# Combining two expert outputs a token: weighted sums on TensorE through diagonal matrices instead of on VectorE

## Chip, core and metric

The kernel runs on one NeuronCore of a Trainium2 chip. The metric is the device time of one execution in microseconds (us). A tile is 128 tokens on the 128 partitions; there are eight tiles of 128 x 1024 fp32 values.

## The reference, cut to what matters

A decoder trunk of two layers works on 1024 tokens of width 1024. Each layer has a token mixer (a gated delta rule in layer 0, differential attention in layer 1) and then a mixture of experts, in which every token goes to two of 32 experts. Behind each comes a layer norm of the scaled residual stream:

```python
ALPHA = (2 * DEPTH) ** 0.25
def layer_norm(x, g, b):
    mu = jnp.mean(xf, axis=-1, keepdims=True)
    var = jnp.mean(jnp.square(xf - mu), axis=-1, keepdims=True)
    return ((xf - mu) * lax.rsqrt(var + LN_EPS) * g + b).astype(x.dtype)
...
    y = jax.ops.segment_sum(y_rows * row_gate[:, None], row_tok, num_segments=n)
...
    ffn = hierarchical_moe(h, moe_w_group[layer], moe_w_expert[layer], moe_w13[layer], moe_w2[layer])
    h = layer_norm(ALPHA * h + ffn, ln_ffn_g[layer], ln_ffn_b[layer])
```

For a token with the expert rows y0 and y1 and the gates g0 and g1 the part around the change computes layer_norm(ALPHA * h + g0 * y0 + g1 * y1).

## The kernel before

The program runs layer 0's mixer and experts, then `combine` (L1796) for layer 0, then the projections and the attention of layer 1, its output projection and experts, and at the very end `combine` for layer 1, whose output is the kernel's. The experts write their rows to a buffer `y` in HBM (two rows a token) by indirect DMA; an overflow loop behind them (L1769), whose number of trips is read at run time, ends every engine's work of the stage. `combine` starts behind it.

For each tile `combine` loads `yin`, the two expert rows of its tokens (1 MB, on SyncE's queue, three tiles ahead in layer 0, all eight in layer 1: `YB`), and for the later tiles the residual `h`. `first` has ScalarE multiply y0 by its gate (L1823); VectorE adds ALPHA * h (L1826) and then g1 * y1 (L1827), all in SBUF. `normalize` takes the statistics on VectorE (two `bn_stats` L245, `bn_aggr` L247), the reciprocal standard deviation on ScalarE with six activations of one column (`rstd`, L232 to L237: a logarithm and an exponential among them), and two passes: way 0 has both on VectorE (L258, L263); way 1 has the first on VectorE (L258), the scaling on ScalarE (L260) and the addition on GpSimd (L261); way 2 has one pass on ScalarE (L254) and two on GpSimd (L255, L256). `WAYS` gives the way of each tile: in layer 0 six tiles of way 1 and two of way 0; in layer 1 ways 1 and 2 in turn, then two of way 0.

ScalarE evaluates functions from a table, which an ACT_TABLE_LOAD brings in. `preload_act_table_set` (L1825) loads the set that holds both logarithm and exponential. Where an activation's set isn't known to be there, the compiler puts a load of its own ahead of it, on the activation's line.

In layer 0 each finished tile is stored to HBM (L1833) and also transposed: TensorE transposes it in eight pieces into PSUM (`ctr`, L1839), ScalarE copies them to `hT` (L1842), rounded, and VectorE writes the remainder (L1843). From tile 2 on `c.bp.start` begins projection units of layer 1 (`pj`, three matmuls in a row, L223 to L225, from `hT` and the split weights `wh` and `wl`), whose matmuls stand between the transposes on TensorE. The third unit is the first that needs all eight tiles of `hT`. A scheduler writes each engine's order at build time; each engine works its row in order.

Of the kernel before, what the change touches and what calls it, by code (L numbers as in the profile page):

```python
# [9 lines left out]
F32 = mybir.dt.float32  # L10
# [4 lines left out]
AF = mybir.ActivationFunctionType  # L15
OP = mybir.AluOpType
AX = mybir.AxisListType
PSUM = bass.MemoryType.PSUM

P = 128  # L20
D = 1024
T = 1024
KT = 8
NT = 8
# [3 lines left out]
ALPHA = 4.0 ** 0.25  # L28
# [23 lines left out]
CAH = 1  # L52

HA = ((2, 5), (2, 5))
YB = (3, 8)
LGT = 1
WAYS = ((1,) * 6 + (0,) * 2, (1,) * 6 + (0,) * 2, (1,) * 6 + (0,) * 2, (1, 2, 1, 2, 1, 2, 0, 0))
WB = 2
CAPS = (
    (96, 96, 80, 128, 128, 112, 112, 104, 96, 96, 88, 88, 80, 80, 80, 80) + (64,) * 8 + (56,) * 3 + (48,) * 5,  # L60
# [70 lines left out]
def instruction(i):  # L131
    return getattr(i, "ins", i)


def row_bc(ap, n):
    return bass.AP(tensor=ap.tensor, offset=ap.offset, ap=[[0, P], [1, n]])
# [91 lines left out]
def rstd(c, sd, mv):  # L228

    act = c.nc.scalar.activation  # L230
    r, v, w = (sd[:, i:i + 1] for i in range(3))
    act(w, mv[:, 1:2], AF.Ln, bias=c.ln_eps, scale=1.0)  # L232
    act(v, mv[:, 1:2], AF.Identity, bias=c.half_eps, scale=-0.5)
    act(r, w, AF.Exp, scale=-0.5)
    act(w, r, AF.Square)
    act(w, w, AF.Identity, bias=c.three_half, scale=v)  # L236
    act(r, r, AF.Copy, scale=w)  # L237


def normalize(c, lp, a, lg, lb, way):  # L240

    nc = c.nc
    st = lp.tile([P, 2, 6], F32, name="ln_st")
    for k in range(2):
        nc.vector.bn_stats(st[:, k, :], a[:, k * 512:(k + 1) * 512])  # L245
    mv = lp.tile([P, 2], F32, name="ln_mv")
    nc.vector.bn_aggr(mv, st)  # L247
    sd = lp.tile([P, 4], F32, name="ln_sd")
    rstd(c, sd, mv)
    r, m = sd[:, 0:1], sd[:, 3:4]  # L250
    if way == 2:
        nc.scalar.activation(m, mv[:, 0:1], AF.Copy, scale=-1.0)
        nc.scalar.activation(m, m, AF.Copy, scale=r)
        nc.scalar.activation(a, a, AF.Identity, scale=r, bias=m)  # L254
        nc.gpsimd.tensor_tensor(a, a, lg, OP.mult)  # L255
        nc.gpsimd.tensor_tensor(a, a, lb, OP.add)  # L256
        return
    nc.vector.scalar_tensor_tensor(a, a, mv[:, 0:1], lg, op0=OP.subtract, op1=OP.mult)  # L258
    if way == 1:
        nc.scalar.activation(a, a, AF.Copy, scale=r)  # L260
        nc.gpsimd.tensor_tensor(a, a, lb, OP.add)  # L261
    else:
        nc.vector.scalar_tensor_tensor(a, a, r, lb, op0=OP.mult, op1=OP.add)  # L263
# [573 lines left out]
def out_proj(c, res, part, layer, h_dram):  # L837
# [4 lines left out]
    with ExitStack() as es:  # L842
# [41 lines left out]
        def norm(n, t, a):  # L884
            normalize(c, lp, a, lg, lb, WAYS[layer][n])
            nc.sync.dma_start(h_dram[t * P:(t + 1) * P], a)
# [909 lines left out]
def combine(c, layer, h_dram, y_dram, dst, hT=None):  # L1796

    nc, tc, ins = c.nc, c.tc, c.ins
    with ExitStack() as es:
        yp = es.enter_context(tc.tile_pool(reuse_waits="tile", name="c_y", bufs=YB[layer]))  # L1800
        lp = es.enter_context(tc.tile_pool(reuse_waits="tile", name="c_l", bufs=3))
        ps = es.enter_context(tc.tile_pool(reuse_waits="tile", name="c_ps", bufs=2, space=PSUM))
        lg, lb = c.w.tile(), c.w.tile()
        c.h += [c.w.spare() for t in range(HA[layer][1], NT)]
        yv = y_dram.rearrange("(t p k) f -> t p k f", p=P, k=2)

        ys = []

        def load(t):

            ys.append(yp.tile([P, 2, D], F32, name="yin"))
            with tc.issue_after(c.load0) if t else ExitStack():
                c.load0 = instruction(nc.sync.dma_start(ys[t], yv[t]))
                if t == LGT:
                    nc.sync.dma_start(lg, row_bc(ins["ln_ffn_g"][layer], D))
                    nc.sync.dma_start(lb, row_bc(ins["ln_ffn_b"][layer], D))
                if t >= HA[layer][1]:
                    nc.sync.dma_start(c.h[t], h_dram[t * P:(t + 1) * P])

        def first(t):  # L1820
            n = TILES[layer].index(t)
            y, a = ys[t], c.h[t]
            nc.scalar.activation(y[:, 0], y[:, 0], AF.Copy, scale=c.gates[:, n, 0:1])  # L1823
            if t == 0:
                tc.keep_in_program_order(nc.scalar.preload_act_table_set("natural_log_exp_and_others"))  # L1825
            nc.vector.scalar_tensor_tensor(a, a, ALPHA, y[:, 0], op0=OP.mult, op1=OP.add)  # L1826
            nc.vector.scalar_tensor_tensor(a, y[:, 1], c.gates[:, n, 1:2], a, op0=OP.mult, op1=OP.add)  # L1827
            return t, a

        def second(t, a):  # L1830
            normalize(c, lp, a, lg, lb, WAYS[2 + layer][t])
            store = nc.gpsimd if layer == 0 and WAYS[2][t] else nc.sync
            store.dma_start(dst[t * P:(t + 1) * P], a)  # L1833
            if hT is not None:
                for gr in range(2):
                    pt = ps.tile([P, 4, P], F32, name="ctr")
                    for i in range(4):
                        k = gr * 4 + i
                        nc.tensor.transpose(pt[:, i], a[:, k * P:(k + 1) * P], c.ident)  # L1839
                    sl = slice(t * P, (t + 1) * P)  # L1840
                    kk = slice(gr * 4, gr * 4 + 4)
                    nc.scalar.copy(hT[0][:, kk, sl], pt)  # L1842
                    nc.vector.tensor_tensor(hT[1][:, kk, sl], pt, hT[0][:, kk, sl].bitcast(F32), OP.subtract)  # L1843


        for t in range(NT):
            while len(ys) < min(NT, t + YB[layer]):
                load(len(ys))
            second(*first(t))
            if layer == 0 and t >= WB:  # L1850
                c.bp.start(t - WB)
    c.raw2.close()
# [25 lines left out]
def build(c, out):  # L1878
    nc, tc = c.nc, c.tc
    with ExitStack() as es:  # L1880
# [11 lines left out]
        with ExitStack() as ws:  # L1892
            phase_a(c, ws, p1, h1)
            with ExitStack() as ms:
                experts_open(c, ms)
                routing(c, 0)
                c.first_b = [c.ins["w_kvq"][i] for i in (0, 16, 8)]
                experts(c, 0, h1, y1)
            bs = es.enter_context(ExitStack())
            hp = bs.enter_context(tc.tile_pool(reuse_waits="tile", name="hT", bufs=1))  # L1900
            hT = [hp.tile([P, KT, T], F32R, tag=f"hT{i}", name=f"hT{i}") for i in range(2)]
            ps = bs.enter_context(ExitStack())
            phase_b_open(c, ps)
            combine(c, 0, h1, y1, h2, hT)
        phase_b_attention(c, hT, hp, h2, p2)
        ps.close()
        with ExitStack() as ws:
            weights_open(c, 1, ws)
            out_proj(c, h2, p2, 1, h3)
            bs.close()  # L1910
            with ExitStack() as ms:
                experts_open(c, ms)
                routing(c, 1)
                experts(c, 1, h3, y2)
            combine(c, 1, h3, y2, out)
# [18 lines left out]
```

## Time and profile before

| | before |
|---|---|
| median of 3 runs | 2745.63 us (2743.77 to 2754.32) |
| profiled execution | 2752.11 us, of which span 2750.3 us |
| mean granted TensorE clock of it | 0.931 |
| TensorE busy | 2366.5 us, 86% of the span |
| VectorE busy | 1503.0 us, 55% |
| ScalarE busy | 1214.9 us, 44% |
| GpSimd busy | 545.2 us, 20% |
| stretch of `combine`, layer 0 | about 1364 to 1444 us |
| stretch of `combine`, layer 1 | about 2688 us to the end |

In the rows PE is TensorE, DVE is VectorE, ACT is ScalarE, POOL is GpSimd, SP is SyncE. A row of a timeline has the start, the duration (both in us, from the span's start), engine, line, operation and tiles written and read; xN joins N instructions. In brackets stands the idle time ahead of it and what ended that. The clock is a share of 2.4 GHz: 1.00 is 2.4 GHz and 0.50 is 1.2 GHz. An fp32 matmul leaves two records.

### The profile page before, as it was taken

The numbers are of one execution on the slowest core, as the hardware profiler recorded it, in microseconds if no ns is written. First come the engines' busy times: TensorE is split into PE (matmuls) and PEld (weight loads), VectorE is DVE, ScalarE is ACT, GpSimd is POOL, SyncE is SP. The second block draws the span as 40 slices with busy tenths as digits, with TensorE's granted clock in tenths as the row PEclk, the third lists the DMA queues.
The fourth block names the chain that finished last, engine by engine and source line by source line (L and its number), as shares of the span: only waits on it lengthen the run. The fifth ranks groups of instructions, "written<-read, shape, count | busy, mean of one in ns | idle before, by whom it ended". The sixth has DMA issues, their size and how long they took to land. (4 is left out here: it accounts for less than half of the span.)

```text
span 2750.3 us, 40132 instructions
## 1 busy us (share of the span) xinstructions
PE 2366.5 (86%) x14447; PEld 1645.2 (60%) x14447; DVE 1503.0 (55%) x2710; ACT 1214.9 (44%) x2187; POOL 545.2 (20%) x445
## 2 busy tenths in 40 slices
PE   8999999998979989898649999999886796779990
PEld 5777777776745544444238777777664373455560
DVE  4555555564556555455295667667535422334467
ACT  5355555543325444444255555556332322223454
POOL 3333333331212111010042111111012111111104
PEclk9999999999979999999859999999987898899995
DMA  4111111124678999999951110101445969799995
GB/s 145 51 59 51 55 59 47 58 75 123 242 274 302 394 388 381 383 380 384 351 210 35 39 33 31 39 26 61 155 170 210 393 250 363 288 381 362 362 366 230
DMA packets 195484, 564.09 MB, mean 205 GB/s; under 512 B 40400, under 2 KB 63184, under 8 KB 193232
## 3 DMA queue, kind: packets, MB, share of 16 engines
q1 hardware_dynamic: 178240, 515.07, 51.0%
q0 software_dynamic: 15168, 43.01, 4.5%
q10 hardware_dynamic: 1872, 3.40, 0.4%
q8 instruction: 115, 1.88, 0.3%
q14 instruction: 89, 0.73, 0.1%
HBM read 515.58 MB, written 52.89 MB: 207 GB/s over the span
## 5 line engine op out<-in xcount | busy, mean ns | idle before, releaser
L210 DVE TENSOR_TENSOR ml<-mraw,mh 128x1024 fp32r<-128x1024 f32 x300 | 357.0, 1222 | 289.4 <-ACT mh L210 270.5
L210 ACT CAST mh<-mraw 128x1024 fp32r<-128x1024 f32 x300 | 306.7, 1052 | 281.7 <-DMA mraw<-in_w 226.1
L210 PE MATMUL acc<-mh,xT 128*128 128x512 f32 (+5 forms) x976 | 331.8, 409 | 1.6 <-ACT mh L210 1.6
L210 PE MATMUL acc<-mraw,xTw 128*32 128x256 f32 (+1 forms) x1632 | 241.4, 500 | 18.7 <-DVE xTw L210 10.1
L185 POOL TENSOR_TENSOR wl<-raw,wh 128x512 fp32r<-128x512 f32 x106 | 155.0, 1482 | 485.1 <-ACT wh L184 420.9
L210 PEld LDWEIGHTS acc<-mh,xT 128*128 128x128 f32 (+5 forms) x976 | 168.4, 173 | 88.3 <-issue 17.1
L223 PE MATMUL pj<-xh,wh 128*128 128x512 f32 x512 | 218.2, 426 | 0.0
L224 PE MATMUL pj<-xl,wh 128*128 128x512 f32 x512 | 209.6, 409 | 0.0
L225 PE MATMUL pj<-xh,wl 128*128 128x512 f32 x512 | 207.9, 406 | 0.4 <-POOL wl L185 0.4
L1584 POOL DMA_INDIRECT X<-h,xidx x69 | 71.0, 1029 | 651.1 <-PE mtw L210 339.0
L210 PE MATMUL acc<-ml,xT 128*128 128x512 f32 (+5 forms) x496 | 198.4, 404 | 0.8 <-DVE ml L210 0.8
L223 PE MATMUL pj<-hT,wh 128*128 128x512 f32 (+1 forms) x432 | 164.8, 381 | 9.1 <-DVE kll L1010 5.7
L224 PE MATMUL pj<-hT,wh 128*128 128x512 f32 (+1 forms) x432 | 166.9, 386 | 0.0
L225 PE MATMUL pj<-hT,wl 128*128 128x512 f32 (+1 forms) x432 | 161.2, 373 | 2.1 <-POOL wl L185 2.1
L210 PE MATMUL acc<-mh,hT 128*128 128x512 f32 (+5 forms) x480 | 158.4, 401 | 0.1
L210 PE MATMUL acc<-mraw,hTw 128*32 128x256 f32 (+1 forms) x816 | 129.3, 540 | 30.4 <-ACT hTw L210 23.9
L210 PEld LDWEIGHTS acc<-mraw,xTw 128*32 128x32 f32 (+1 forms) x1632 | 71.4, 124 | 127.8 <-issue 71.2
L408 DVE SCALAR_TENSOR_TENSOR cv<-pr,cw,cv 128x512 f32<-128x512 f32 x144 | 119.0, 826 | 51.2 <-ACT cv L405 49.1
L1114 ACT ACTIVATE e<-sc,sm 128x256 f32<-128x256 f32 (+7 forms) x128 | 94.6, 742 | 89.7 <-DVE sm L1112 89.3
L225 PEld LDWEIGHTS pj<-xh,wl 128*128 128x128 f32 x512 | 97.2, 190 | 20.1 <-POOL wl L185 0.9
L210 PEld LDWEIGHTS acc<-mh,hT 128*128 128x128 f32 (+5 forms) x480 | 82.2, 172 | 44.6 <-issue 10.5
L224 PEld LDWEIGHTS pj<-xl,wh 128*128 128x128 f32 x512 | 97.7, 191 | 18.1 <-issue 1.7
(407 smaller groups left out, 4917.7 us busy)
## 6 DMA issues: line engine op xcount, KB each, us to landing
mraw<-in_w SPq DMA_DIRECT2D x720, 512.0 KB, 10.7
raw<-in_w_in SPq DMA_DIRECT2D x32, 512.0 KB, 3.7
yin<-y SPq DMA_DIRECT2D x16, 1024.0 KB, 6.9
raw<-in_w_kvq SPq DMA_DIRECT2D x21, 512.0 KB, 3.6
h<-res SPq DMA_DIRECT2D x16, 512.0 KB, 3.9
p<-ores POOLq DMA_DIRECT2D x12, 512.0 KB, 4.8
res<-p SPq DMA_DIRECT2D x12, 512.0 KB, 5.8
mh<-in_w SPq DMA_DIRECT2D x12, 512.0 KB, 8.1
```

The lines of the kernel that those rows point to most:

```text
L185: c.nc.gpsimd.tensor_tensor(l[:, s], src[:, s], h[:, s].bitcast(F32), OP.subtract)
L210: out = getattr(self.engine, name)(*args, **kwargs)
L223: mm(out, ah, bh, start=first, stop=False)
L224: mm(out, ah, bl, start=False, stop=False)
L225: mm(out, al, bh, start=False, stop=last)
L408: nc.vector.scalar_tensor_tensor(a, pr[:, 1 + j:513 + j], cw[:, idx, j:j + 1], a, op0=OP.mult, op1=OP.add)
L1114: nc.scalar.activation(e[:, 0:L], st[m][:, 0:L], AF.Exp, bias=sm[:, 2 + m:3 + m], scale=SC, accum_out=sm[:, 4 + m:5 + m])
L1584: c.last_gather = instruction(nc.gpsimd.indirect_dma_start(out=b.X[0:rows], out_offset=None, in_=h_dram, in_offset=bass.IndirectOffsetOnAx ...
```

## The change

`first` no longer multiplies and adds on ScalarE and VectorE. A tile `diag` holds seventeen 128 x 128 diagonal matrices: one for each gate column of each tile, made by VectorE from the identity and the gates in two instructions (L1816), and one with ALPHA on its diagonal, made by ScalarE (L1811). TensorE multiplies diag(g0) with y0 and diag(g1) with y1 in fp32 and accumulates both in a PSUM tile `sum` (L1840). For tiles 0 and 1 (`RESP`) the residual is a third product in the same accumulation, with the ALPHA matrix; for the other six VectorE adds ALPHA * h in place in PSUM (L1854). `normalize` takes the statistics and the first pass from PSUM (`src`). `yin` is two half tiles, so that each half is a transfer of 512 KB, and `YB` counts halves: two tiles ahead in layer 0, all in layer 1. Layer 1's `WAYS` become those of layer 0. `sum` has two buffers in layer 0 and four in layer 1; `ctr` uses a pool of the projection. The table preload stands once, behind the ALPHA matrix (L1812). In the changed kernel `rstd`, `normalize` and the lines that other functions have there stand three or four lines further down.

```diff
-YB = (3, 8)
+YB = (4, 16)
...
-WAYS = ((1,) * 6 + (0,) * 2, (1,) * 6 + (0,) * 2, (1,) * 6 + (0,) * 2, (1, 2, 1, 2, 1, 2, 0, 0))
+WAYS = ((1,) * 6 + (0,) * 2, (1,) * 6 + (0,) * 2, (1,) * 6 + (0,) * 2, (1,) * 6 + (0,) * 2)
+
+RESP = ((1, 1, 0, 0, 0, 0, 0, 0), (1, 1, 0, 0, 0, 0, 0, 0))
+SUMS = (2, 4)
...
-def normalize(c, lp, a, lg, lb, way):
+def normalize(c, lp, a, lg, lb, way, src=None):
 
     nc = c.nc
+    src = a if src is None else src
     st = lp.tile([P, 2, 6], F32, name="ln_st")
     for k in range(2):
-        nc.vector.bn_stats(st[:, k, :], a[:, k * 512:(k + 1) * 512])
+        nc.vector.bn_stats(st[:, k, :], src[:, k * 512:(k + 1) * 512])
...
-    nc.vector.scalar_tensor_tensor(a, a, mv[:, 0:1], lg, op0=OP.subtract, op1=OP.mult)
+    nc.vector.scalar_tensor_tensor(a, src, mv[:, 0:1], lg, op0=OP.subtract, op1=OP.mult)
...
-        ps = es.enter_context(tc.tile_pool(reuse_waits="tile", name="c_ps", bufs=2, space=PSUM))
+        dp = es.enter_context(tc.tile_pool(reuse_waits="tile", name="c_d", bufs=1))
+        ps = es.enter_context(tc.tile_pool(reuse_waits="tile", name="c_ps", bufs=SUMS[layer], space=PSUM))
         lg, lb = c.w.tile(), c.w.tile()
+
+        diag = dp.tile([P, 2 * NT + 1, P], F32, name="diag")
+        nc.scalar.activation(diag[:, 2 * NT], c.ident, AF.Copy, scale=ALPHA)
+        tc.keep_in_program_order(nc.scalar.preload_act_table_set("natural_log_exp_and_others"))
+        gates = c.gates.rearrange("p t k -> p (t k)")
+        for q in (slice(0, 4), slice(4, 2 * NT)):
+            n = q.stop - q.start
+            nc.vector.tensor_tensor(diag[:, q], c.ident[:, None, :].to_broadcast([P, n, P]),
+                                    gates[:, q, None].to_broadcast([P, n, P]), OP.mult)
...
-            ys.append(yp.tile([P, 2, D], F32, name="yin"))
+            ys.append([yp.tile([P, D], F32, name="yin") for k in range(2)])
             with tc.issue_after(c.load0) if t else ExitStack():
-                c.load0 = instruction(nc.sync.dma_start(ys[t], yv[t]))
+                for k in range(2):
+                    c.load0 = instruction(nc.sync.dma_start(ys[t][k], yv[t][:, k]))
...
+        sums = {}
+
+        def add(t, w, src, start, stop):
+            for f in range(2):
+                h = slice(f * 512, (f + 1) * 512)
+                nc.tensor.matmul(sums[t][:, h], diag[:, w], src[:, h], start=start, stop=stop)
+
+        def residual(t):
+
+            if t < NT:
+                sums[t] = ps.tile([P, D], F32, name="sum")
+                if RESP[layer][t]:
+                    add(t, 2 * NT, c.h[t], True, False)
+
         def first(t):
             n = TILES[layer].index(t)
-            y, a = ys[t], c.h[t]
-            nc.scalar.activation(y[:, 0], y[:, 0], AF.Copy, scale=c.gates[:, n, 0:1])
-            if t == 0:
-                tc.keep_in_program_order(nc.scalar.preload_act_table_set("natural_log_exp_and_others"))
-            nc.vector.scalar_tensor_tensor(a, a, ALPHA, y[:, 0], op0=OP.mult, op1=OP.add)
-            nc.vector.scalar_tensor_tensor(a, y[:, 1], c.gates[:, n, 1:2], a, op0=OP.mult, op1=OP.add)
-            return t, a
-
-        def second(t, a):
-            normalize(c, lp, a, lg, lb, WAYS[2 + layer][t])
+            for k in range(2):
+                add(t, 2 * n + k, ys[t][k], k == 0 and not RESP[layer][t], k == 1)
+            if not RESP[layer][t]:
+                nc.vector.scalar_tensor_tensor(sums[t], c.h[t], ALPHA, sums[t], op0=OP.mult, op1=OP.add)
+
+        def second(t):
+            a = c.h[t]
+            normalize(c, lp, a, lg, lb, WAYS[2 + layer][t], sums[t])
...
-                    pt = ps.tile([P, 4, P], F32, name="ctr")
+                    pt = c.bp.ps.tile([P, 4, P], F32, tag="tr", name="ctr")
...
+        for t in range(SUMS[layer]):
+            residual(t)
         for t in range(NT):
-            while len(ys) < min(NT, t + YB[layer]):
+            while len(ys) < min(NT, t + YB[layer] // 2):
                 load(len(ys))
-            second(*first(t))
+            first(t)
+            second(t)
+            residual(t + SUMS[layer])
```

The order of the instructions changes at three places. The first is ScalarE in layer 1, before the change, behind the overflow loop: one table load, the products, and the six activations of the first tiles.

```order
L1823 ACTIVATE yin<-yin,gates 128x1024
L1825 ACT_TABLE_LOAD
L1823 ACTIVATE yin<-yin,gates 128x1024
L232 ACTIVATE ln_sd<-ln_mv,ct_all 128x1
L233 ACTIVATE ln_sd<-ln_mv,ct_all 128x1
L234 ACTIVATE ln_sd<-ln_sd 128x1
```

In the changed kernel the row of ScalarE ahead of that loop, in the last expert (`sil`, `silw`, `hT`, `ysb` and `yw` are its tiles), now holds the ALPHA matrix and the preload, and the last silu has a load:

```order
L213 ACTIVATE sil<-acc 88x512
L213 CAST hT<-mtr 128x4x88
L1811 ACTIVATE diag<-ct_all 128x128
L1812 ACT_TABLE_LOAD
L1766 DMA mraw<-h_65 128x1024 x2
L213 COPY ysb<-acc 88x512
L1766 DMA mraw<-h_65 128x1024
L213 ACT_TABLE_LOAD
L213 ACTIVATE silw<-acc 128x128
```

Behind the loop the first tile and the start of the second stand so in the changed kernel, with a load ahead of the logarithm (L235) and one ahead of the exponential (L237); the other six tiles repeat it, the last two without L264:

```order
L235 ACT_TABLE_LOAD
L235 ACTIVATE ln_sd<-ln_mv,ct_all 128x1
L236 ACTIVATE ln_sd<-ln_mv,ct_all 128x1
L237 ACT_TABLE_LOAD
L237 ACTIVATE ln_sd<-ln_sd 128x1
L238 ACTIVATE ln_sd<-ln_sd 128x1
L239 ACTIVATE ln_sd<-ln_sd,ct_all 128x1
L240 ACTIVATE ln_sd<-ln_sd 128x1
L264 ACTIVATE mraw<-mraw,ln_sd 128x1024
L235 ACT_TABLE_LOAD
```

The preload has moved from behind the loop to ahead of it, and sixteen loads stand behind it. In layer 0 the preload stayed behind the loop, and no other load is there. The second place is TensorE in layer 0, in the changed kernel; `sum` are the new sums (one row is one fp32 matmul, xN joins N), `ctr` the transposes and `pj` the projection units. Before, only the transposes stood there among the unit's matmuls.

```order
L1840 MATMUL sum<-mraw,diag 128x512 x4
L1840 MATMUL sum<-yin,diag 128x512 x11
L1866 MATMUL ctr<-ct_all,mraw 128x128 x8
L1840 MATMUL sum<-yin,diag 128x512 x4
L1866 MATMUL ctr<-ct_all,mraw 128x128 x8
L1840 MATMUL sum<-yin,diag 128x512
L226 MATMUL pj<-hT_12017,wh 128x256
L227 MATMUL pj<-hT_12018,wh 128x256
```

So the sums of a later tile stand ahead of an earlier tile's transposes, and a part of tile 3's sums ahead of the first unit. The third place is VectorE in layer 1, in the changed kernel, for tiles 0 to 2:

```order
L249 BN_STATS ln_st<-sum 128x6 x2
L251 BN_AGGR ln_mv<-ln_st 128x2
L262 SCALAR_TENSOR_TENSOR mraw<-sum,ln_mv,mraw 128x1024
L249 BN_STATS ln_st<-sum 128x6 x2
L251 BN_AGGR ln_mv<-ln_st 128x2
L262 SCALAR_TENSOR_TENSOR mraw<-sum,ln_mv,mraw 128x1024
L1854 SCALAR_TENSOR_TENSOR sum<-mraw,sum 128x1024
L249 BN_STATS ln_st<-sum 128x6 x2
```

The two summing passes are gone, and from tile 2 on the residual pass (L1854) stands ahead of the statistics.

## Rows read from the trace of the kernel before

**Rows 1.** Windows: length; busy (x instructions) by engine; TensorE clock, DMA share, GB/s.

```profile
1364.00:1390.00 26.00, 3.93 (x16) 3.13 (x16) 18.36 (x23) 13.86 (x26) 6.40 (x4) 0.50 0.88 331
1390.00:1397.10 7.10, 4.87 (x21) 4.58 (x22) 7.10 (x6) 5.43 (x11) 5.36 (x3) 0.50 0.55 193
1397.10:1407.40 10.30, 5.33 (x37) 4.28 (x36) 10.30 (x11) 6.38 (x14) 6.04 (x5) 1.00 0.98 336
1407.40:1441.50 34.10, 11.50 (x48) 9.69 (x49) 32.52 (x40) 16.69 (x43) 12.86 (x9) 0.50 0.36 136
2694.00:2720.00 26.00, 0.00 (x0) 0.00 (x0) 24.07 (x23) 15.42 (x30) 11.62 (x4) 0.50 0.99 406
```

**Rows 2.** The timeline of layer 0's ends (start, duration): ScalarE, VectorE, TensorE.

```profile
1370.33 1.28 ACT L1825 ACT_TABLE_LOAD   x1
1371.65 1.15 ACT L1823 ACTIVATE yin<-yin,gates 128x1024 f32<-128x1024 f32 x1
...
1437.83 1.28 DVE L263 SCALAR_TENSOR_TENSOR mraw<-mraw,ln_sd 128x1024 f32<-128x1024 f32 x1
...
1443.75 0.28 PE L223 MATMUL pj<-hT,wh 128*128 128x256 f32 x1
```

**Rows 3.** VectorE's groups by line, 1364 to 1444 (busy and mean, idle before).

```profile
L258 DVE SCALAR_TENSOR_TENSOR mraw<-mraw,ln_mv 128x1024 f32<-128x1024 f32 x8 | 16.9, 2118 | 0.1
...
L1826 DVE SCALAR_TENSOR_TENSOR mraw<-mraw,yin 128x1024 f32<-128x1024 f32 x8 | 13.8, 1731 | 5.1 <-ACT yin L1823 5.1
L1827 DVE SCALAR_TENSOR_TENSOR mraw<-yin,gates,mraw 128x1024 f32<-128x1024 f32 x8 | 13.4, 1688 | 0.1
```

**Rows 4.** The timeline of VectorE at the start of layer 1.

```profile
2694.85 1.23 DVE L1826 SCALAR_TENSOR_TENSOR mraw<-mraw,yin 128x1024 f32<-128x1024 f32 x1 [10.99 <-ACT yin L1823]
...
2697.43 1.29 DVE L245 BATCH_NORM_STATS2 ln_st<-mraw 128x6 f32<-128x512 f32 x2
...
2699.76 0.20 DVE L247 BATCH_NORM_AGGREGATE ln_mv<-ln_st 128x2 f32<-128x12 f32 x1
```

**Rows 5.** The timeline of VectorE, then GpSimd, in layer 0.

```profile
1379.33 3.28 DVE L258 SCALAR_TENSOR_TENSOR mraw<-mraw,ln_mv 128x1024 f32<-128x1024 f32 x1
...
1385.10 1.29 DVE L1843 TENSOR_TENSOR hT<-ctr,hT 128x512 fp32r<-128x512 f32 x2
...
1379.18 2.34 POOL L261 TENSOR_TENSOR mraw<-mraw 128x1024 f32<-128x1024 f32 x1 [20.92 <-DMA yin<-y]
...
1384.45 2.83 POOL L261 TENSOR_TENSOR mraw<-mraw 128x1024 f32<-128x1024 f32 x1 [2.00 <-ACT mraw L260]
```

**Rows 6.** The timeline of TensorE at one fp32 matmul, and the window around it.

```profile
158.23 1.02 PE L699 MATMUL pr<-sq,ct_all 128*128 128x512 f32 x2
159.09 0.38 PE L680 MATMUL sc<-qd,S 128*128 128x128 f32 x2
...
158.20:159.10 0.90, 0.90 (x5) 0.36 (x5) 0.87 (x4) 0.90 (x3) 0.64 (x1) 1.00 0.00 0
```

**Rows 7.** The instructions of line L700 (ns: shortest, median, longest).

```profile
L700 ACT ACT_TABLE_LOAD  x16: 1283/1283/1283, 160.2 to 674.8; - x16
```

**Rows 8.** The timeline of ScalarE in layer 1, and its scaling pass by line.

```profile
2700.00 0.30 ACT L232 ACTIVATE ln_sd<-ln_mv,ct_all 128x1 f32<-128x1 f32 x1 [2.69 <-DVE ln_mv L247]
...
2701.26 0.30 ACT L237 ACTIVATE ln_sd<-ln_sd 128x1 f32<-128x1 f32 x1
...
L260 ACT ACTIVATE mraw<-mraw,ln_sd 128x1024 f32<-128x1024 f32 x3 | 3.4, 1148 | 4.7 <-DVE mraw L258 4.7
```

**Rows 9.** The timeline around the end of the last expert: ScalarE, VectorE, SyncE.

```profile
2678.86 0.28 ACT L210 ACTIVATE silw<-acc 128x128 f32<-128x128 f32 x1 [0.88 <-PE acc L210]
...
2678.01 0.69 DVE L210 COPY ysb<-acc 88x512 f32<-88x512 f32 x1 [7.82 <-ACT ysb L210]
...
2688.86 0.80 SPq L1813 DMA_DIRECT2D yin<-y  x2
```

**Rows 10.** The timeline of VectorE at the end of the program.

```profile
2745.31 1.28 DVE L263 SCALAR_TENSOR_TENSOR mraw<-mraw,ln_sd 128x1024 f32<-128x1024 f32 x1 [0.31 <-ACT ln_sd L237]
```

More of the change, by code (lines that the diff above doesn't have):

```diff
@@ L253, in normalize @@
         nc.scalar.activation(m, m, AF.Copy, scale=r)
-        nc.scalar.activation(a, a, AF.Identity, scale=r, bias=m)
+        nc.scalar.activation(a, src, AF.Identity, scale=r, bias=m)
         nc.gpsimd.tensor_tensor(a, a, lg, OP.mult)
```

## The prediction

> **What bounds the kernel now.** TensorE is busy 86% of the span, but a share over the program says nothing about the two stretches that change, so I read those by windows [rows 1]. The first call (layer 0) lies at 1364 to 1442 us. There VectorE is busy 18.36 + 7.10 + 10.30 + 32.52 = 68.3 of 77.5 us, without a break in the middle windows, while TensorE works 3.93 + 4.87 + 5.33 + 11.50 = 25.6 us. In the second call (layer 1, the end of the program) VectorE works 24.07 of the 26 us from 2694 to 2720, TensorE nothing, and DMA is full (0.99). So VectorE sets the pace of both calls. In layer 0 it is 9.3 us a tile: the first product of ScalarE ended at 1370.3 (it takes 1.15 us, so 1369.2 is its start), and the third projection unit, which needs the whole of hT, started at 1443.75 [rows 2].
>
> The groups by line say what VectorE does [rows 3]: two passes that sum (13.8 + 13.4 us over eight tiles), the statistics, and the first pass of the norm (16.9 us, 2118 ns each). A summing pass takes 1.23 us where GpSimd is quiet [rows 4]. Beside GpSimd's addition the passes stretch: the L258 that began at 1379.33, 0.15 us after GpSimd's pass of 2.34 us, took 3.28 us, whereas the pair L1843, which reads one operand from PSUM, kept 1.29 us for both although GpSimd worked from 1384.45 to 1387.28 [rows 5].
>
> **The change, layer 1.** Removed: the product on ScalarE (a pass of L260's form, 1148 ns) and both summing passes on VectorE. Added for a tile: four fp32 matmuls of 128x512, which are eight records. The nearest row is L699, the same shape and type: two records fill 158.23 to 159.09 at the full clock, 0.43 us each [rows 6]. Eight are 3.44 us, and 6.9 us at half the clock. VectorE keeps the statistics (1.29 + 0.20 us [rows 4]) and the first pass, now read from PSUM, and in six tiles gets the residual pass, PSUM + SBUF to PSUM. No row shows that form. Its bounds are 1.23 us (L1826 unstretched) and 2.1 us (the stretched mean); I take 1.3, twice an L1843, the only row that mixes the two memories. With 1.28 for the first pass that is 1.29 + 0.20 + 1.28 + 1.30 less overlaps = 3.9 us a tile, of the size of TensorE's 3.44.
>
> What decides is ScalarE, and the order shows why: in layer 1 the single table load moved ahead of the last expert's silu, which now loads a table of its own, and behind the overflow loop each of the eight tiles has one load before the logarithm and one before the exponential, sixteen in all. Before, one load served them all. A load took 1283 ns each of 16 times at L700 [rows 7], and behind the one at 1370.33 the next pass began 0.04 us after its end [rows 2]. So a way-1 tile costs ScalarE two loads, 2.57 us; the six small activations, 1.56 (2700.00 to 2701.56); and the scaling pass, 1.15 [rows 8]. With 0.1 for gaps that is 5.4 us. It is more than VectorE's 3.9, so the tables set the pace.
>
> The Trainium skill ("ScalarE: Activation LUTs", What ACT_TABLE_LOAD costs) gives a load the same time and adds a drain of about 1.38 us to every switch. The trace doesn't show that drain behind the load at 1370.33. By that page sixteen switches would cost 22 us more than I count.
>
> The chain: the silu's own load delays the last expert. ScalarE waited 0.88 us for that silu's input [rows 9], so between 0.4 us (most of the load in the wait) and 1.28; I take 1.2, since the copies ahead of it keep ScalarE until shortly before. The first y transfer then starts at 2690.1 instead of 2688.86. Now VectorE's first pass began at 2694.85, behind a product of 1.15, so y was there 4.8 us after the issue: 2694.9 in the changed kernel. The second half is summed by four records, cold, 3.4 us later, and statistics take 1.5: 2699.8, so I say 2700, the same as now (the first logarithm started at 2700.00 [rows 8]). From there ScalarE: six tiles of 5.4, less the first load, which lies in the wait, make 31.1; two tiles without the scaling pass, 4.2 each, make 8.4: 2739.5. The last pass on VectorE takes 1.28 us as now, and from its end to the span's end it was 2750.3 - 2746.6 = 3.7 us [rows 10]: 2744.5. **Layer 1 gains 5.8 us.** Bounds: if loads cost nothing, VectorE's pace applies (2700 + 2.6 + 6 x 3.9 + 3 + 3.7 = 2732.7), a gain of 17; at half the clock TensorE's eight tiles take 55 us from 2694.9, and statistics, the last tile's activations with two loads, the last pass and the store add 9.5: 2759.4, a loss of 9. GpSimd's one pass of 2.34 to 2.83 us in 5.4 is hidden. The diagonal matrices (VectorE 2048 columns, 2.5 us at L1826's rate, ScalarE one short pass) stand ahead of the loop beside the last expert, where VectorE waits 7.82 us at a stretch [rows 9]: nothing; uncovered they would cost those 2.5 us.
>
> **Layer 0.** Here the preload stays behind the loop and replaces the load at 1370.33 and one before it; both lay in the wait for y, so nothing is won. Off VectorE come 13.8 + 13.4 us, and, if the first pass from PSUM stretches no more than L1843 did, 16.9 - 8 x 1.28 = 6.7. On it come six residual passes, 7.8. That leaves 68.3 - 33.9 + 7.8 = 42.2 us, 5.3 a tile. TensorE gets 3.44 or 6.9 us a tile beside its present 25.6 / 8 = 3.2, most of which ran at 1.2 GHz (clock 0.50 [rows 1]) and would take about half of it at 2.4: 5.0 us a tile warm, 10.1 cold. Cold, TensorE is the new bound; warm, it is level with VectorE. The diagonals and the residuals of tiles 0 and 1 run while y is awaited.
>
> First sums done: 1369.2 + 6.9 (cold) = 1376.1. Then seven tiles. Behind the last sum: statistics, first pass and activations 3.3 us, and from the last tile's last pass to the third unit 1443.75 - 1437.83 = 5.9, as now [rows 2]. All warm: 1376.1 + 7 x 5.3 + 9.2 = 1422.4, 21 us earlier; all cold: 1456.0, 12 us later. So the clock decides. Now it rose to 1.00 at 1397.1, behind 7.1 us in which TensorE worked 4.87, and was back at 0.50 from 1407.4, with 11.50 of 34.1 us worked [rows 1]. With the sums TensorE has a larger part of the stage to work than in the 7.1 us ahead of that rise, but not from the first tile on, so I take three tiles cold and four warm: 1436.8, 7 us earlier. I take 2 off again, since the second unit's matmuls stand between the sums in TensorE's row and wait for weights to be split; the sums queue behind them. **Layer 0 gains 5 us**, bounds a gain of 21 and a loss of 12. With half tiles, y is fetched two tiles ahead instead of three, and SyncE waits for TensorE's sums instead of L1827. At 331, 193 and 136 GB/s against 406 in layer 1 [rows 1] transfers have room on the whole: nothing.
>
> **Sum.** 5.8 + 5 = 10.8 us off the profiled execution's 2752.1, of which 2750.3 is span. That execution lies 6.5 above the median of the runs shown, so from 2745.6 I predict 2735 us. Half a per cent, about what a measurement of this kernel can tell from no change, is 13.7 us.
>
> **The rivals.**
> - TensorE warm early in layer 0, so that its gain comes in full (21 + 5.8): 2719 us. For it: the sums are dense. Against it: the clock stood at 0.50 for most of that stretch.
> - Slower: TensorE stays at 1.2 GHz in both calls. Layer 0 loses 12 and layer 1 loses 9: 2767 us. For it: in layer 1 the clock is 0.50 with TensorE idle [rows 1], and each call begins cold. A loss of over half a per cent needs nearly all sixteen tiles cold, since a warm one gives back 4.8 or 3.4 us. Against it: eight times 6.9 us is denser than what went before the rise at 1397.1. The Trainium skill ("TensorE: Matmul & The Clock Gate", What's actually happening) has an idle array at 1.2 GHz and the clock following activity; the rows agree.
> - Nothing won in layer 0, since the third unit waits for something else, its split weights: 2740 us. Against it: every unit's matmuls read hT, which the last tile completes.
> - Every table load with a drain: 22 us more on ScalarE's chain, 2757 us. Against it: the 0.04 us at 1371.65 [rows 2].
>
> **How the numbers follow.** My forecast 0.5, its own range 2730 to 2744 (between two and five of layer 0's seven tiles cold); warm early 0.25; slow clock 0.10; nothing in layer 0 0.12; drains 0.03. Faster by over 0.5% (under 2732): the warm case and a seventh of the forecast, 0.32. Slower (over 2759): the slow clock, 0.10. Between: 0.58. For 8 in 10 the range goes from 2720, near the warm case, to 2754, leaving out the slow clock and the drains.
>
> **What would show it.** Behind the overflow loop of layer 1: sixteen loads of 1283 ns, ScalarE nearly unbroken at 5.4 us a tile, VectorE with gaps that the norm's activations end. Records of the sums 0.43 us apart at clock 1.00 and 0.86 at 0.50. First passes near 1.28 us beside GpSimd's additions. The third unit's start near 1438. I would be wrong if the loads cost less or more than 1.28 us, if passes from PSUM took clearly over 1.3 us, or if the clock fell between the sums.

## The result, and the profile after

| | before | after |
|---|---|---|
| median | 2746.65 us (2743.77 to 2754.32, 7 runs) | 2733.75 us (2725.63 to 2736.67, 7 runs) |
| ratio | | 0.9942, 95% interval 0.9929 to 0.9955 |
| profiled execution: span, clock | 2750.3 us, 0.931 | 2726.5 us, 0.950 |
| first y transfer of layer 0 issued | 1364.1 us | 1353.8 us |
| from there to the end of the last hT subtraction | 78.4 us | 67.2 us |
| from there to the first y transfer of layer 1 | 1324.7 us | 1314.5 us |
| from that to the end of the span | 61.4 us | 58.2 us |

The change makes the kernel 0.6% faster, 12.9 us by the medians. The two profiled spans differ by 23.8 us, and 10.3 of these lie ahead of the first changed instruction: the first y transfer of layer 0 was issued at 1364.1 in the one and at 1353.8 in the other. Over all thirteen other profiles of this study it lies between 1353.8 and 1360.5, so the profile of before was late there for a reason outside the change. What the change did is therefore read from distances inside the two stretches, not from the spans.

Windows of the kernel after, laid like those of [rows 1] (length; busy and instructions of TensorE, its weight loads, VectorE, ScalarE, GpSimd; clock; DMA share; GB/s). The first three are layer 0, the last two layer 1:

```profile
1350.00:1359.40 9.40, 5.87 (x7) 2.52 (x8) 3.28 (x9) 1.79 (x3) 0.15 (x1) 0.51 0.60 190
1359.40:1367.00 7.60, 7.51 (x18) 3.04 (x16) 2.84 (x5) 1.78 (x7) 0.00 (x0) 1.00 0.96 368
...
1383.00:1400.00 17.00, 15.63 (x58) 8.54 (x58) 11.93 (x18) 9.95 (x25) 11.51 (x8) 0.90 0.77 274
...
2681.00:2700.00 19.00, 19.00 (x46) 8.36 (x45) 17.17 (x24) 18.29 (x33) 7.05 (x3) 1.00 1.03 411
...
2705.00:2727.00 22.00, 0.00 (x0) 0.00 (x0) 6.29 (x7) 14.46 (x26) 4.67 (x2) 0.56 0.24 96
```

Before, TensorE worked 3.93 of layer 0's first 26 us, at clock 0.50 [rows 1]; now it is at 1.00 from 1359.4 to 1383, and at 0.90 on average in the 17 us that follow. No engine is full from end to end of layer 0: TensorE comes nearest, with 15.63 of 17 us. In layer 1 ScalarE works 18.29 of 19 us from 2681 to 2700, and from 2705 on VectorE works 6.29 of 22 us. Before, it had little rest at the end of the program:

```profile
2720.00:2751.00 31.00, 0.00 (x0) 0.00 (x0) 26.25 (x25) 13.54 (x39) 15.35 (x5) 0.50 0.26 103
```

The passes on VectorE and GpSimd in layer 0, by line, answer to [rows 3]:

```profile
L265 POOL TENSOR_TENSOR mraw<-mraw 128x1024 f32<-128x1024 f32 x6 | 14.0, 2341 | 23.4 <-ACT mraw L264 23.4
...
L262 DVE SCALAR_TENSOR_TENSOR mraw<-sum,ln_mv,mraw 128x1024 f32<-128x1024 f32 x8 | 10.2, 1279 | 0.2
...
L1854 DVE SCALAR_TENSOR_TENSOR sum<-mraw,sum 128x1024 f32<-128x1024 f32 x6 | 7.3, 1221 | 2.9 <-PE sum L1840 2.9
```

The first pass takes 1279 ns now (2118 before), although GpSimd works beside it, and GpSimd's own pass 2341 ns. The residual pass, whose form no row of before showed, takes 1221.

ScalarE in layer 1, tiles 0 and 1, and the last tile:

```profile
2680.38 1.28 ACT L237 ACT_TABLE_LOAD   x1
2681.67 0.20 ACT L237 ACTIVATE ln_sd<-ln_sd 128x1 f32<-128x1 f32 x1
...
2684.06 1.28 ACT L235 ACT_TABLE_LOAD   x1
2685.35 0.29 ACT L235 ACTIVATE ln_sd<-ln_mv,ct_all 128x1 f32<-128x1 f32 x1
...
2718.47 0.29 ACT L235 ACTIVATE ln_sd<-ln_mv,ct_all 128x1 f32<-128x1 f32 x1 [1.50 <-DVE ln_mv L251]
```

Two loads stand in every tile, and the logarithm of tile 1 (2685.35) comes 5.47 us behind that of tile 0 (2679.88). The activation behind the load at 2680.38 begins 0.01 us after its end. Only the last tile waits for VectorE, 1.50 us. On VectorE the same stretch is idle:

```profile
2704.80 1.22 DVE L1854 SCALAR_TENSOR_TENSOR sum<-mraw,sum 128x1024 f32<-128x1024 f32 x1
2715.71 1.28 DVE L267 SCALAR_TENSOR_TENSOR mraw<-mraw,ln_sd 128x1024 f32<-128x1024 f32 x1 [9.69 <-ACT ln_sd L240]
2716.91 1.29 DVE L249 BATCH_NORM_STATS2 ln_st<-sum 128x6 f32<-128x512 f32 x2
...
2721.48 1.28 DVE L267 SCALAR_TENSOR_TENSOR mraw<-mraw,ln_sd 128x1024 f32<-128x1024 f32 x1 [1.73 <-ACT ln_sd L240]
```

Its last residual pass was done at 2706.0. Then it waited 9.69 us for ScalarE's chain of tile 6, with the statistics of tile 7 behind the waiting pass in its row, although tile 7's sum was there.

### The profile page after: what moved, and what is told of

Same layout as the page of the kernel before. It is cut to its first block, busy times and chain, and to the rows that moved or that the text cites. A ratio compares the mean times of both kernels' runs of the same rounds, so it can differ in the third digit from the quotient of the medians.

```text
span 2726.5 us, 40436 instructions
## 1 busy us (share of the span) xinstructions
PE 2420.8 (89%) x14591; PEld 1663.5 (61%) x14591; DVE 1465.4 (54%) x2697; ACT 1216.9 (45%) x2183; POOL 525.7 (19%) x442
## 5 line engine op out<-in xcount | busy, mean ns | idle before, releaser
L213 PE MATMUL acc<-mraw,xTw 128*32 128x256 f32 (+1 forms) x1632 | 247.9, 510 | 24.9 <-DVE xTw L213 17.7
L213 PE MATMUL acc<-mraw,hTw 128*32 128x256 f32 (+1 forms) x816 | 119.1, 510 | 21.1 <-ACT hTw L213 14.4
## 6 DMA issues: line engine op xcount, KB each, us to landing
mraw<-in_w SPq DMA_DIRECT2D x720, 512.0 KB, 10.7
```

Of the source, the lines that this page charges most:

```text
L213: out = getattr(self.engine, name)(*args, **kwargs)
```

## The experiments

All times are ratios to the kernel before, run on the same chip. Two distances are read from each profile: "hT" is from the first y transfer of layer 0 to the end of the last hT subtraction, "end" is from the first y transfer of layer 1 to the end of the span.

**One load in layer 1.** My theory: the table loads pace layer 1. The rival: they lie in waits that exist anyway.

```diff
-        tc.keep_in_program_order(nc.scalar.preload_act_table_set("natural_log_exp_and_others"))
+        if layer == 0:
+            tc.keep_in_program_order(nc.scalar.preload_act_table_set("natural_log_exp_and_others"))
...
+            if layer == 1 and t == 0:
+                mark = lp.tile([P, 1], F32, name="mark", bufs=1)
+                nc.scalar.copy(mark, ys[0][0][:, 0:1])
+                tc.keep_in_program_order(nc.scalar.preload_act_table_set("natural_log_exp_and_others"))
```

> The changed kernel with the preload of layer 1 behind the overflow loop (a one-column copy of the first y half stands ahead of it, so that the scheduler can't hoist it), which leaves one load there instead of sixteen and none ahead of the last silu. If the table loads set the pace of layer 1, ScalarE's 5.47 us a tile falls to about 2.8 and VectorE's 3.9 us takes over: VectorE's last residual pass was issued at 2704.8, so the end comes about 12 us earlier, and 1 us more without the silu's load: 13 us less than the changed kernel, 0.989 to 0.991 of the kernel before. If the loads lie in waits that exist anyway, the time is that of the changed kernel, 0.994.

Measured: 2724.52 us, 0.992 (0.9907 to 0.9932), 9.2 us under the changed kernel's median. "End" is 47.3 us instead of 58.2, and the silu's load is gone too. That is 10.9 + 1.3 = 12.2 us by the stretches, as expected; the total shows 6 us by the ratios (each against runs of the kernel before made beside it) and 9 by the medians; the interval of one ratio is some 7 us wide. ScalarE's and then VectorE's rows of that run:

```profile
2676.96 1.28 ACT L1881 ACT_TABLE_LOAD   x1
...
2705.66 0.29 ACT L235 ACTIVATE ln_sd<-ln_mv,ct_all 128x1 f32<-128x1 f32 x1 [0.64 <-DVE ln_mv L251]
...
2710.71 1.47 DVE L267 SCALAR_TENSOR_TENSOR mraw<-mraw,ln_sd 128x1024 f32<-128x1024 f32 x1
...
2715.25 1.28 DVE L267 SCALAR_TENSOR_TENSOR mraw<-mraw,ln_sd 128x1024 f32<-128x1024 f32 x1 [0.30 <-ACT ln_sd L240]
```

One load lies in the wait for y, ScalarE's logarithms wait for VectorE's aggregates, and the last pass is 4.5 us behind that of tile 6, where it was 5.8. ScalarE no longer sets the pace, and the theory holds. VectorE has few gaps left, but whether it is the pace now is another question, which the run with the old ways (below) answers otherwise.

**The change in layer 0 alone, and in layer 1 alone.** The other layer keeps the old `combine`, which stands in the program as `combine_old`.

```diff
# layer 0 alone
-            combine(c, 1, h3, y2, out)
+            combine_old(c, 1, h3, y2, out)
# layer 1 alone
-            combine(c, 0, h1, y1, h2, hT)
+            combine_old(c, 0, h1, y1, h2, hT)
```

> The change in layer 0 alone; layer 1 keeps the old combine. If most of the gain is in layer 0 (TensorE warm, the sums off VectorE), the ratio to the kernel before is about 0.996 (11 us). If layer 0 gains only the 5 us that I predicted, 0.998; if the gain is in layer 1, 1.000.

> The change in layer 1 alone; layer 0 keeps the old combine. By the two traces layer 1 gained 3.2 us behind the first y transfer and lost 1.2 us ahead of it: about 2 us, ratio 0.999. By my prediction 5.8 us, 0.998. If the gain were mostly here, 0.995.

Measured: layer 0 alone 0.9965 (0.9951 to 0.9979), with hT 64.5 and end 61.3 us; layer 1 alone 0.9987 (0.9978 to 0.9996), with hT 78.1 and end 58.4 us. So some 9.6 us come from layer 0 and 3.6 from layer 1, and the sum of the two is the change's 0.9942 within the intervals.

**No residual on TensorE.** To see whether the products that run while y is awaited are what warms TensorE.

```diff
-RESP = ((1, 1, 0, 0, 0, 0, 0, 0), (1, 1, 0, 0, 0, 0, 0, 0))
+RESP = ((0, 0, 0, 0, 0, 0, 0, 0), (0, 0, 0, 0, 0, 0, 0, 0))
```

> The changed kernel with all residuals on VectorE (no products with the ALPHA matrix). If the residual products of tiles 0 and 1, which run while y is awaited, are what brings TensorE to the full clock before the first sums, then the first sums of layer 0 run at half the clock (8 records 6.9 us instead of 3.5) and the third unit starts 3 to 6 us later: 0.995 to 0.997 of the kernel before. If the clock rises just as early without them, only two passes of 1.23 us come to VectorE in each layer, and the ratio stays at 0.994.

Measured: 2736.68 us, 0.9966 (0.9953 to 0.9979), but hT 67.1 and end 58.2 us, as in the changed kernel. The windows at the start of its layer 0:

```profile
1357.50:1365.00 7.50, 3.56 (x5) 1.53 (x6) 2.41 (x8) 0.76 (x2) 0.00 (x0) 0.50 0.82 271
1365.00:1372.00 7.00, 6.22 (x15) 2.59 (x14) 4.97 (x6) 2.10 (x7) 0.00 (x0) 1.00 0.94 355
```

At half the clock it is only until about 1365, which lies within tile 0's sums (they begin at 1361.4), and from there it is at 1.00. So the residual products bring the clock up earlier, as the first branch of the expectation had it, but hT doesn't come later without them. For the 0.0024 in the total neither stretch has a place. The same edit was tried again on top of one load:

> The kernel with one load, with all residuals on VectorE in both layers. Without table loads in the way, both layers show what the residual products are worth. The run without them and with sixteen loads was at 0.9966 against 0.9942, though its two stretches in the trace were as long as those of the changed kernel (within 1.6 us). If that difference is real, this run comes to 0.994 to 0.995; if it was scatter of the rest of the program, to 0.992, and layer 1 from the first y transfer to the end takes 46 to 49 us (47.3 with residual products).

Measured: 0.9915 (0.9897 to 0.9932), hT 68.4, end 46.9 us. The difference did not come again, so I take it for scatter: against no residual products at all, those of two tiles are worth nothing that these runs can tell.

**Statistics and first pass from SBUF.** With one load, the residual pass of tiles 2 to 7 writes SBUF.

```diff
-                nc.vector.scalar_tensor_tensor(sums[t], c.h[t], ALPHA, sums[t], op0=OP.mult, op1=OP.add)
+                nc.vector.scalar_tensor_tensor(c.h[t], c.h[t], ALPHA, sums[t], op0=OP.mult, op1=OP.add)
...
-            normalize(c, lp, a, lg, lb, WAYS[2 + layer][t], sums[t])
+            normalize(c, lp, a, lg, lb, WAYS[2 + layer][t], sums[t] if RESP[layer][t] else None)
```

> The kernel with one load (the last run but for this edit): the residual pass of tiles 2 to 7 writes SBUF instead of PSUM, so statistics and first pass of six tiles read SBUF; the number of passes is the same. If reading PSUM is what keeps the first pass at 1.28 us beside GpSimd, the first passes in SBUF stretch to 1.7 to 2.1 us where GpSimd works, and layer 1, where VectorE is nearly unbroken, ends 2 to 5 us later: about 0.993 to 0.994 against 0.992. If the source makes no difference, 0.992 and means of 1.28.

Measured: 0.992 (0.9904 to 0.9936), end 51.6 us instead of 47.3, hT 66.9. VectorE's passes in layer 1, by line:

```profile
L262 DVE SCALAR_TENSOR_TENSOR mraw<-mraw,ln_mv 128x1024 f32<-128x1024 f32 x6 | 11.7, 1949 | 0.1
...
L1855 DVE SCALAR_TENSOR_TENSOR mraw<-mraw,sum 128x1024 f32<-128x1024 f32 x6 | 7.2, 1207 | 0.6 <-PE sum L1841 0.6
...
L262 DVE SCALAR_TENSOR_TENSOR mraw<-sum,ln_mv,mraw 128x1024 f32<-128x1024 f32 x2 | 2.6, 1284 | 0.1
```

In the run with one load, where all eight first passes read PSUM and GpSimd's six additions stand beside them as here, the row is this:

```profile
L262 DVE SCALAR_TENSOR_TENSOR mraw<-sum,ln_mv,mraw 128x1024 f32<-128x1024 f32 x8 | 10.2, 1278 | 0.2
```

The same pass takes 1949 ns on average from SBUF (1.27 us where GpSimd was idle, up to 3.20 beside its addition) and 1278 from PSUM, and layer 1 is 4.3 us longer for it. The total doesn't show the 4.3 us; its interval is 8.8 us wide. In layer 0, where the passes stretched to 1563 ns, hT didn't move.

**The kernel before with sixteen loads.**

```diff
-            if t == 0:
+            if t == 0 and layer == 0:
                 tc.keep_in_program_order(nc.scalar.preload_act_table_set("natural_log_exp_and_others"))
```

> The kernel before with the preload of layer 1 left out, so that each tile loads a table before the logarithm and one before the exponential. ScalarE's tile is then 1.15 (product) + 2.57 + 1.56 + 1.2 = 6.5 us against about 5.8 of VectorE (46 us over eight tiles). If loads count in full once ScalarE is the slowest, layer 1 ends 4 to 8 us later: 1.0015 to 1.003. If they lie in waits, 1.000.

Measured: 1.0017 (1.0005 to 1.0028), end 67.5 us instead of 61.4. The loads alone cost the old kernel 6 us. Of these, 3.7 stand in VectorE's waits for the products (the row of L1826 in layer 1; 11.9 us of waiting before) and 1.4 in its wait for the last tiles' standard deviations (1.7 us against 0.3):

```profile
L1826 DVE SCALAR_TENSOR_TENSOR mraw<-mraw,yin 128x1024 f32<-128x1024 f32 x8 | 15.8, 1970 | 15.6 <-ACT yin L1823 15.6
```

**What paces layer 0 now.** Three kernels, each with one load in layer 1, give one resource more or less work in layer 0 (in the third, `twice` is 2 in layer 0).

```diff
# more products
+            if layer == 0 and not RESP[layer][t]:
+                add(t, 2 * n, ys[t][0], True, True)
# half the transfers
-                for k in range(2):
+                for k in range(2 if layer else 1):
                     c.load0 = instruction(nc.sync.dma_start(ys[t][k], yv[t][:, k]))
# statistics twice
-    for k in range(2):
+    for k in [0, 1] * twice:
         nc.vector.bn_stats(st[:, k, :], src[:, k * 512:(k + 1) * 512])
```

> The kernel with one load, and in layer 0 the first gate's product of tiles 2 to 7 done twice (the first is overwritten): four more records a tile, 1.73 us at the full clock, 10.4 us in all. If TensorE is what paces layer 0 now, the last subtraction of hT comes 8 to 10 us later than 66.5 to 69 us behind the first y transfer, and the ratio is 0.995 to 0.996. If VectorE or a transfer paces it, at most 3 us later.

> The kernel with one load; in layer 0 the second expert row of each token isn't loaded, and the first is used for both products, so that y moves 4 MB instead of 8 (the sums, and all behind them, are of other values). All engines do the same work. Two parts of the layer-0 stage could pace it now: transfers (DMA was busy 0.95 to 1.00 of the first 30 us) or the chain of waits from statistics to transposes. If transfers pace it, the last subtraction of hT ends 6 to 10 us earlier than the 64 to 70 us behind the first y transfer, and the ratio is 0.989; if the chain does, it stays within 2 us and the ratio at 0.992.

> The kernel with one load, and in layer 0 every tile's statistics taken twice (the same values): 1.3 us more of VectorE a tile, 10.4 in all. Before the change VectorE paced that stage. If it still does, the last subtraction of hT ends 8 to 10 us later and the ratio is 0.9955; if VectorE has been taken off the path, at most 4 us later, 0.992 to 0.9935.

With unchanged code in layer 0, hT was 67.2, 64.5, 69.6, 63.8 and 66.0 us in five profiles, 66.2 on average. More products: hT 67.7 us, 0.9913 (0.9898 to 0.9928). Half the transfers: 67.8 us, 0.991 (0.9895 to 0.9924). Statistics twice: 73.0 us, 0.9935 (0.9921 to 0.9949). The second window (30 to 70 us behind the first y transfer) of the runs with one load, with more products, and with statistics twice:

```profile
1385.30:1425.30 40.00, 30.04 (x131) 18.85 (x132) 29.31 (x46) 21.19 (x55) 15.51 (x12) 0.84 0.57 203
```

```profile
1389.50:1429.50 40.00, 34.22 (x169) 21.95 (x166) 28.46 (x42) 20.63 (x55) 11.61 (x9) 1.00 0.54 196
```

```profile
1388.40:1428.40 40.00, 24.49 (x120) 15.55 (x119) 33.29 (x51) 18.83 (x51) 14.22 (x10) 0.94 0.52 186
```

With more products TensorE took 34.22 of the 40 us. Its last sum ended 56.8 us behind the first y transfer, against 48.4 to 54.2 in the five profiles, and yet hT stayed in their scatter (63.8 to 69.6): TensorE had the room. The added products did not cost their full 10.4 us, though: the clock was 1.00 throughout that window, where it was 0.84 without them. The transfers had room too. Of 10.4 us more on VectorE, 6.8 reached the end of hT, by one profile; that is less than the 8 to 10 expected if VectorE alone set the pace and more than the 4 if it were off the path, and the total (0.9935) lies 4 us above the run with one load, with intervals that overlap. So VectorE is in part on the path that sets the end of layer 0, though it works only 29 of 40 us there.

**Old ways in layer 1, and one residual.** Attempts at a faster version on top of one load; the second has both edits.

```diff
-WAYS = ((1,) * 6 + (0,) * 2, (1,) * 6 + (0,) * 2, (1,) * 6 + (0,) * 2, (1,) * 6 + (0,) * 2)
+WAYS = ((1,) * 6 + (0,) * 2, (1,) * 6 + (0,) * 2, (1,) * 6 + (0,) * 2, (1, 2, 1, 2, 1, 2, 0, 0))
...
-RESP = ((1, 1, 0, 0, 0, 0, 0, 0), (1, 1, 0, 0, 0, 0, 0, 0))
+RESP = ((1, 1, 0, 0, 0, 0, 0, 0), (1, 0, 0, 0, 0, 0, 0, 0))
```

> The kernel with one load, and layer 1's ways as they were before (1,2,1,2,1,2,0,0): three first passes of 1.28 us leave VectorE for ScalarE, which has over 1 us free a tile, and GpSimd gets one more pass of 2.4 us for each. If VectorE paces layer 1 now, it ends 3 to 4 us earlier: 0.9905. If TensorE's sums or the transfers pace it, no change from 0.992; if GpSimd's second pass comes on the path, later.

> The kernel with one load and the old ways in layer 1, and there only tile 0's residual on TensorE instead of two tiles'. In the run with one load the residual products of both tiles held TensorE from 2673.6 to 2679.5, while y's first half was there at 2676.8. One tile's products end at about 2676.7, so the first sums start 2.7 us earlier, at half the clock for longer. If the start counts, layer 1 ends 1 to 3 us earlier: 0.9905 to 0.991; if the transfers or VectorE's further pass of 1.22 us count, no change from 0.9915.

Measured: 0.9915 (0.9901 to 0.993), end 46.7 us; and 0.9919 (0.9904 to 0.9934), end 46.4 us. Three first passes taken off VectorE gave 0.6 us instead of 3 to 4, and the earlier start 0.3 us more: neither can be told from the kernel with one load. So VectorE alone doesn't pace layer 1 there. TensorE's sums run without a break to the same point in both: the rows are of the run with one load, of the old ways, and (three rows) of one residual.

```profile
2679.46 27.63 PE L1841 MATMUL sum<-yin,diag 128*128 128x512 f32 x64
```

```profile
2679.37 27.63 PE L1841 MATMUL sum<-yin,diag 128*128 128x512 f32 x64
```

```profile
2675.43 3.78 PE L1841 MATMUL sum<-mraw,diag 128*128 128x512 f32 x4 [7.00 <-issue]
2679.01 7.32 PE L1841 MATMUL sum<-yin,diag 128*128 128x512 f32 x16
2687.04 20.87 PE L1841 MATMUL sum<-yin,diag 128*128 128x512 f32 x48 [0.71 <-DMA yin<-y]
```

With one residual tile 0's sum was done 8.1 us behind the first y transfer instead of 10.1, but ahead of tile 2 TensorE waited 0.71 us for y, and the last sum ended 33.2 us behind that transfer, against 34.1 and 33.8 in the other two. Whether the sums or the transfers set the end was not tried apart. All versions with one load stand at 0.991 to 0.992 of the kernel before where nothing was added, ahead of the change's 0.9942.

## Why the prediction was right

The forecast was 2735 us, a gain of 10.8; measured were 2733.75 and 12.9. The sum came out, its two terms less well: I had 5.8 us in layer 1 and 5 in layer 0, and the stretches show about 2 and 11. That the sum came so near is luck in part: the 3.9 us too many in the one and the 5.7 too few in the other nearly cancel.

**Layer 1: the mechanism was right, and the start and the last tile were mis-sized.** ScalarE's tile was forecast at 5.4 us and takes 5.47; sixteen loads of 1283 ns stand where the order had them. With one load the stretch falls by 10.9 us, where I had put the bound of free loads 11.8 us below the forecast (2744.5 - 2732.7). The "end" stretch won 3.2 us and the silu's load took 1.3 back, so 1.9 of the 5.8:

```profile
2658.36 1.28 ACT L213 ACT_TABLE_LOAD   x1 [0.81 <-PE acc L213]
...
2679.88 0.29 ACT L235 ACTIVATE ln_sd<-ln_mv,ct_all 128x1 f32<-128x1 f32 x1 [10.14 <-DVE ln_mv L251]
...
2668.30 1.75 SPq L1828 DMA_DIRECT2D yin<-y  x4
```

The silu's load began only after the wait of 0.81 us, so it costs its full 1.28 (I had 1.2). The first logarithm came 11.6 us behind the first y transfer, where I had 9.9. The residual products hold TensorE for 5.7 us of that, at half the clock at first:

```profile
2668.98 5.86 PE L1840 MATMUL sum<-mraw,diag 128*128 128x512 f32 x8 [6.05 <-issue]
2674.68 20.76 PE L1840 MATMUL sum<-yin,diag 128*128 128x512 f32 x48
```

The step that failed is "the second half is summed by four records, cold, 3.4 us later". It lets the first half's four records be done when the second half lands (5.1 us behind the first issue, by the trace). In the changed kernel the residual products stand in their way until 2674.68, and all eight come behind them, warm: tile 0's sum is complete 10.0 us behind the issue (2678.31 - 2668.30), where I had 8.2. I had put the residual products at nothing. Without any (two runs) the first sum began 3.8 us behind the issue, but at half the clock, and was complete at 10.1: eight cold records behind the first half give 3.8 + 6.9, near that. With one tile's alone (one run, on top of one load) it began at 4.3 and was complete at 8.1. Of the other 2 us, 1.50 are those of the last tile, which I had not seen: its statistics stand in VectorE's row behind a pass that waits for ScalarE. The rest is small differences, of 0.07 us in each tile among them.

**Layer 0: right in sign, and mis-sized by half.** By five profiles with the new `combine` in layer 0 and three with the old one, the distance to layer 1's first transfer is 1314.7 us instead of 1325.4 (1.3 us taken off where a silu load lies in it): a gain of 10.7 us, with single profiles up to 3 us to either side. The term that failed is "three tiles cold and four warm". TensorE was warm before the first sum, and the first sixteen records took 0.44 us each. Once the clock fell between the sums, which I had named as a sign of being wrong: it was 0.50 from 1383.1 to 1386.5, behind two waits of TensorE for the units' weights (1.66 and 0.85 us), and six records took 4.37 us where six warm ones take 2.83:

```profile
1359.88 7.03 PE L1840 MATMUL sum<-yin,diag 128*128 128x512 f32 x16
...
1383.27 4.37 PE L1840 MATMUL sum<-yin,diag 128*128 128x512 f32 x6
...
1396.57 2.83 PE L1840 MATMUL sum<-yin,diag 128*128 128x512 f32 x6
```

So the "warm early" rival had the clock right but for those 1.5 us. It was not its 21 us that came, though, but 11. Its sum put the third unit 58.3 us behind the first y transfer (1422.4 - 1364.1); it started 67.6 behind it (1421.44 - 1353.80), where my own forecast, near 1438, was 74. Two terms make the difference:

```profile
1401.15 4.46 PE L1840 MATMUL sum<-yin,diag 128*128 128x512 f32 x10
...
1405.64 1.23 DVE L1854 SCALAR_TENSOR_TENSOR sum<-mraw,sum 128x1024 f32<-128x1024 f32 x1 [0.36 <-PE sum L1840]
1408.22 1.29 DVE L1870 TENSOR_TENSOR hT<-ctr,hT 128x512 fp32r<-128x512 f32 x2 [1.35 <-ACT hT L1869]
...
1416.27 1.28 DVE L267 SCALAR_TENSOR_TENSOR mraw<-mraw,ln_sd 128x1024 f32<-128x1024 f32 x1
...
1421.44 0.56 PE L226 MATMUL pj<-hT,wh 128*128 128x256 f32 x1
```

The seven tiles behind the first took 6.0 us each instead of 5.3, which is 5 us. And from the last sum (1405.6) to the last pass (1416.27) lie 10.7 us, where I had 3.3 for tile 7's own statistics, first pass and activations: VectorE's row still held the passes of tiles 6 and 7 and hT subtractions there, and it was idle for little more than the 1.35 us. That is 7 us, and the same 10.7 stands in all five profiles. The first sums were 2.3 us earlier than I had them. Why a tile takes 6.0 us is less clear: I let either VectorE's or TensorE's busy time set the pace, and from 1366 to 1421 neither is full (40.8 and 42.7 of 55 us). The waits there (who waited for whom: us in total, times, longest; the 14.6 is the wait for tile 0) show where the engines stood:

```profile
POOL mraw L265 <- ACT mraw L264: 23.4, 5, 14.6
ACT hT L1869 <- PE ctr L1866: 11.4, 6, 3.2
DVE hT L1870 <- ACT hT L1869: 8.9, 7, 4.0
...
ACT wh L187 <- DMA mraw<-in_w_kvq: 4.3, 2, 2.3
```

Each tile goes from VectorE to ScalarE, GpSimd, TensorE, ScalarE and back to VectorE. The units' weight casts stand between in the rows of ScalarE and GpSimd, and the units' matmuls in TensorE's. By the three runs above VectorE is on the path in part, and neither the transfers nor some 6 us more of sums move its end. That this round through the engines sets the 6.0 us is read from the waits and not shown by a run; which of the casts costs what was not tried.

**VectorE's passes.** That a pass with one operand in PSUM keeps its time beside GpSimd was read from the pair L1843 [rows 5] and is shown by two runs that differ in it (1278 ns with all first passes from PSUM, 1949 from SBUF). It agrees with the Trainium skill ("SBUF — State Buffer", SBUF: two separate sides), by which only VectorE instructions with two SBUF inputs or in a two-port mode contend with GpSimd for a port. The residual pass was taken at 1.3 us and takes 1.22.

**The other rivals.** The slow clock did not come: even without residual products the clock rose to 1.00 while tile 0's eight records ran (5.5 to 6.3 us for the eight, in two runs and both layers). The drain behind a load did not come either: 0.01 us lie between load and activation, and ScalarE's 5.47 us a tile leave no room for 2.8 us more. "Nothing in layer 0" is refuted by the run of layer 0 alone.

## What to carry to other kernels

Read the order on every engine, not only where the diff edits. A table preload without operands can be hoisted past a loop, and then every switch that it was to save comes back. A cast, load or pass is free only in a wait that lasts: the same sixteen loads cost 10.9 us here, where the change had taken work off VectorE, and 6.1 in the kernel before.

Before an engine's busy time is called the pace, compare it with the stage. Where no engine is full, adding to one engine's work tells whether it is on the path (more products: 1.5 of 10.4 us, inside the scatter; statistics twice: 6.8 of 10.4). Look at the clock of such a run too, since the added work can change it.

The end of a stage is not one tile's chain. Count what still stands in each engine's row when the last input comes: here that was 10.7 us instead of 3.3.

## What was not expected of the hardware

Work that runs while data is awaited brought TensorE to 2.4 GHz before the first sum, yet two tiles' residual products were worth nothing in layer 1: they kept TensorE until 6.4 us behind the first y transfer, and the sum was complete no earlier than cold without them. One tile's products (one run, 8.1 us instead of 10.0) gave both, the clock and the early start. GpSimd's addition takes 2341 ns in layer 0, where it took 2876 before. The move of the first pass to PSUM is not the reason, for the addition kept 2357 ns in the run whose first passes read SBUF; the summing passes, which are gone in both, may be, and that was not tried. And the unchanged part ahead of layer 0's `combine` differed by 10 us between the two profiles, which is nearly as much as the change is worth.
